# A decoder layer with sparse attention: DRAM scratch of queries, keys and compression in plain rows, keys stored once, the compression's places as extra matmul columns

## The chip, the core and the metric

One Trainium2 chip, of which the kernel uses one core. The metric is device time in microseconds (us) of one execution; the kernel before was timed in three runs. A profile of one more execution, taken by the hardware profiler, gives the rows below.

## The reference, cut to what matters

One decoder layer on 1024 tokens of width 1024: a projection of x to all mixers' inputs, a gated linear recurrence, a sparse attention with three branches, a gated merge, layer norm, a feed-forward part. The change touches the attention's inputs. Queries have 16 heads of 64; keys and values have 4 heads ("kv"), each for a group of 4 query heads. Queries and the three kinds of keys are rotated by position (rope), which mixes the two halves of 32 in each head. The compressed branch takes blocks of 32 tokens, 16 apart, adds a learned place to each token of the block and runs the block through a small network:

```python
def compress(t, pos_emb, w1, b1, w2, b2):
    ...
    blk = t[:, idx] + pos_emb[None, None, :, None, :]
    blk = blk.transpose(0, 1, 3, 2, 4).reshape(B, n_cmp, H, CMP_LEN * d)
    hdn = jax.nn.silu(blk @ w1 + b1)
    return hdn @ w2 + b2
```

It runs once for the keys (kind 0, on rotated keys) and once for the values (kind 1, not rotated).

## The kernel before, in words

All matmuls of the projections keep near-float32 precision by splitting each operand into a high and a low part of a reduced type: `split` (line 128) casts to the high part on ScalarE (ACT, line 118) and subtracts on VectorE (DVE, line 126); `mm3` (lines 142 to 145) then runs three matmuls, high by high, low by high and high by low. TensorE is PE; PEld are its weight loads.

**Phase 0** (to about 365 us) projects everything that is rotated or compressed. Activations are held transposed as `xh`, `xl`. `pair` loads one weight chunk of 1 MB (tile `w`, two buffers) and splits it to `wh`, `wl` (two buffers each). `rope` (line 273) makes, for each half of 512 tokens, two result tiles `pa` and `pb` of 24 matmuls each (first and second halves of the heads; two buffers each), four products with cosine and sine on VectorE (lines 283 to 286), two sums on GpSimd (POOL, lines 287 and 288), and hands the results to a sink:
- `sink_q` (line 298) splits them and stores four tiles `rh` of 256 KB to `Qd`. The 128 partitions of a tile are 4 heads by 32; in DRAM `Qd` is ordered kv, then 128 rows, then head, so the DRAM side of a store is a pattern of 4 x 32 x 512.
- `sink_k` (line 305) does the same for keys to `Kd`, ordered by kv, and stores each tile twice, so that a later load finds the key in both halves of the 128 partitions. The DRAM pattern is again 4 x 32 x 512, and one rotation makes 16 stores.
- `sink_c` puts the compression's input into `krt` in blocks; `compress_relay` (line 330) stores it to the scratch `Rd`, in four pieces of 256 KB for each kind (DRAM patterns 4 x 32 x 512 for kind 0, 2 x 64 x 512 for kind 1).

The compression of one kind has two halves a (first and second 16 tokens of a block). `compress_keys(kind, a)` (line 356) loads all of `Rd[kind]` (1 MB) into `kr`, adds the places of half a on VectorE (line 364, four instructions), and splits `kr` to `kh` and `kl`. `compress_hidden` (line 371) loads and splits half of the first weights and runs 48 matmuls of 256 columns into the result tiles `hps`. `compress_end` adds the bias, applies the activation and the second matmul. Each of `kr`, `kh`, `kl` has one buffer.

The order of phase 0 is written out (lines 441 to 483): values' and keys' compression inputs, keys(1, 0), rotation of the window keys kw, hidden(1, 0), keys(1, 1), rotation of the selected keys ks, hidden(1, 1), keys(0, 0), queries of kv 0, end(1), hidden(0, 0), keys(0, 1), gates, values vs, hidden(0, 1), values vw, end(0), queries of kv 1 to 3. That is the order of priority; the order on each engine's queue is then planned by the framework, which simulates the program with assumed durations. Every engine works its queue in order. All transfers are issued on the sync engine (SP), in order too: `dma` (line 135) for loads and `dmo` (line 140) for stores.

**Phase 1** (to about 1480 us) runs 32 attention units (4 kv by 8 tiles of 128 queries). `load_kv` (line 732) loads keys `K` (for each of two branches a tile of 128 partitions by 2 x 1024, in two transfers) and values `V` for one kv; `unit` (line 745) loads its queries `Q` (256 KB, two buffers) and computes scores `sc` (line 785). A filler puts the recurrence's matmuls (`pj`) between the units; its first part, `recurrence_values`, stores tiles `it` to `Id`. The tiles of phase 1 use memory that phase 0 releases. **Then** follow the merge, the output projection, norms and the feed-forward part.

Of the kernel before, what the change touches and what calls it, by code (L numbers as in the profile page):

```python
# [9 lines left out]
F32 = mybir.dt.float32  # L10
F32R = mybir.dt.float32r
I32 = mybir.dt.int32
AF = mybir.ActivationFunctionType
OP = mybir.AluOpType
AX = mybir.AxisListType

S = 1024
D = 1024
KT = D // 128
ST = S // 128  # L20
KV = 4
G = 4
# [87 lines left out]
def body(tc, xT, xS, pos, csa, csb, wA, wB, wG, lbl, normg, kpos, kw1, kb1, kw2, kb2, vpos, vw1, vb1,  # L110
# [17 lines left out]
    def split(hi, lo, src, e1="act", e2="dve"):  # L128

        copy(e1, hi, src)  # L130
        sub(e2, lo, src, hi.bitcast(F32))
# [5 lines left out]
    def dmo(o, i):  # L137

        o, i = (t.bitcast(F32) if t.dtype == F32R else t for t in (o, i))
        nc.sync.dma_start(o, i)  # L140

    def mm3(ps, ah, al, bh, bl, start, stop):
        nc.tensor.matmul(ps, ah, bh, start=start, stop=False)  # L143
        nc.tensor.matmul(ps, ah, bl, start=False, stop=False)  # L144
        nc.tensor.matmul(ps, al, bh, start=False, stop=stop)  # L145

    with ctx:
# [5 lines left out]
        nc.vector.memset(powc, -0.5)  # L153


        Qd = dram.tile([KV, 128, G, S], F32, name="Qd")
        Kd = dram.tile([2, KV, 2, 128, S], F32, name="Kd")
        Vd = dram.tile([8, 128, ST, 128], F32, name="Vd")
        Rd = dram.tile([2, 2, 64, KV, 512], F32, name="Rd")
        Id = dram.tile([HH, 128, ST, 128], F32, name="Id")  # L160
        Gd = dram.tile([2, 8, 128, S], F32, name="Gd")
        Md = dram.tile([8, 128, S], F32, name="Md")
# [32 lines left out]
        def pair(name, i=0):  # L195
            return chunk(wpa, wA[PAIRS[name, i]], 256)

        def token_rows(pool, name, w, s2):

            h, l = w  # L200
            p = pool.tile([128, 2, 256], F32, name=name)
            for j in range(2):
                sl = slice((s2 + j) * 128, (s2 + j) * 128 + 128)
                for k in range(KT):
                    mm3(p[:, j], xh[:, k, sl], xl[:, k, sl], h[:, k], l[:, k], k == 0, k == KT - 1)
            return p
# [4 lines left out]
        with p0:  # L211
# [86 lines left out]
            def sink_q(kv):  # L298
                def f(half, y1, y2):
                    sl = slice(half * 512, half * 512 + 512)  # L300
                    for c, y in enumerate(halves(y1, y2)):
                        dmo(Qd[kv, 32 * c:32 * c + 32, :, sl].rearrange("d h s -> h d s"), y)
                return f

            def sink_k(br):
                def f(half, y1, y2):
                    sl = slice(half * 512, half * 512 + 512)
                    for c, y in enumerate(halves(y1, y2)):
                        r0 = 32 * (c % 2)
                        for rep in range(2):  # L310
                            dmo(Kd[br, :, c // 2, r0 + 64 * rep:r0 + 64 * rep + 32, sl], y)
                return f


# [15 lines left out]
            def compress_relay(kind):  # L330

                for j in range(2):
                    for a in range(2):
                        if kind == 0:

                            o = Rd[0, a, 32 * j:32 * j + 32].rearrange("d k x -> k d x")
                        else:

                            o = Rd[1, a, :, 2 * j:2 * j + 2].rearrange("d k x -> k d x")
                        dmo(o, krt[j][:, a].rearrange("p r m -> p (r m)"))  # L340


            CM = [dict(posT=kpos, w1=kw1, b1=kb1, w2=kw2, b2=kb2), dict(posT=vpos, w1=vw1, b1=vb1, w2=vw2, b2=vb2)]
            W = KV * 512

            def compress_begin(kind):
                C = CM[kind]
                C["pt"] = a0.tile([128, 16], F32, name="cpos")
                nc.sync.dma_start(C["pt"], C["posT"])
                C["w2s"] = a0.tile([128, 2, 128], F32, name="w2s")  # L350
                nc.sync.dma_start(C["w2s"], C["w2"])
                C["b1s"] = a0.tile([128, 2], F32, name="b1s")
                nc.sync.dma_start(C["b1s"], C["b1"])
                C["hps"] = [ps0.tile([128, KV * 64], F32, name=f"hps{j}") for j in range(2)]

            def compress_keys(kind, a):

                C = CM[kind]
                kr = c0.tile([128, W + 8], F32, name="kr")
                nc.vector.memset(kr[:, W:], 0.0)  # L360
                nc.sync.dma_start(kr[:, :W], Rd[kind].rearrange("a d k x -> (a d) (k x)"))
                for kv in range(KV):
                    o = kr[:, kv * 512:kv * 512 + 512].rearrange("p (r m) -> p r m", r=8)
                    nc.vector.tensor_tensor(
                        o, o, C["pt"][:, 8 * a:8 * a + 8, None].to_broadcast([128, 8, 64]), op=OP.add)
                kh = c0.tile([128, W + 8], F32R, name="kh")
                kl = c0.tile([128, W + 8], F32R, name="kl")
                split(kh, kl, kr)
                C["k", a] = kh, kl

            def compress_hidden(kind, a):
                C = CM[kind]
                kh, kl = C["k", a]
                wh, wl = chunk(wpa, C["w1"][:, 8 * a:8 * a + 8], 256)

                def rhs(t, r):
                    o = r * 64 + a
                    return bass.AP(tensor=t.tensor, offset=t.offset + o,
                                   ap=[t.ap[0], [512, KV], [1, 64]])

                for r in range(8):
                    for j in range(2):
                        js = slice(j * 128, j * 128 + 128)
                        mm3(C["hps"][j], wh[:, r, js], wl[:, r, js], rhs(kh, r), rhs(kl, r),
                            a == 0 and r == 0, a == 1 and r == 7)

            def compress_end(kind):
# [2 lines left out]
                hid = a0.tile([128, 2, KV * 64], F32, name="hid")  # L390
                for j in range(2):
                    sg = a0.tile([128, KV * 64], F32, name="sg")
                    nc.vector.tensor_scalar(hid[:, j], hps[j], b1s[:, j:j + 1], None, op0=OP.add)
                    nc.scalar.activation(sg, hid[:, j], AF.Tanh, scale=0.5)
                    nc.vector.tensor_scalar(sg, sg, 0.5, 0.5, op0=OP.mult, op1=OP.add)
                    nc.vector.tensor_tensor(hid[:, j], hid[:, j], sg, op=OP.mult)
# [24 lines left out]

            c0 = p0.enter_context(tc.tile_pool(name="c0", bufs=1))


            def gate_chunk():
                w = wpa.tile([128, KT, 128], F32, name="wg", tag="w")
# [20 lines left out]
            rope("kc", 0, sink_c)  # L447
            compress_relay(0)
            compress_begin(1)
            compress_keys(1, 0)  # L450
            rope("kw", 0, sink_k(1))
            compress_hidden(1, 0)
            compress_keys(1, 1)
            rope("ks", 0, sink_k(0))
            compress_hidden(1, 1)
            compress_begin(0)
            compress_keys(0, 0)
            rope("nq", 0, sink_q(0))
            compress_end(1)
            compress_hidden(0, 0)  # L460
            compress_keys(0, 1)

            def values(name, i, evacuate):
                w = pair(name, i)
                for s2 in range(0, ST, 2):
                    evacuate(s2, token_rows(ps0, "pa" if s2 % 4 else "pb", w, s2))

            def sink_v(br):
                def f(s2, p):
                    vt = a2.tile([128, KV, 2, 128], F32R, name="vt", tag="vt", bufs=1)  # L470
                    p_ = p.rearrange("p t (c d) -> p c t d", d=64)
                    split(vt[:, :, :, :64], vt[:, :, :, 64:], p_)
                    dmo(Vd[4 * br:4 * br + 4, :, s2:s2 + 2].rearrange("c p t d -> p c (t d)"),
                        vt.rearrange("p c t d -> p c (t d)"))
                return f

            gate_chunk()
            values("vs", 0, sink_v(0))
            compress_hidden(0, 1)
            values("vw", 0, sink_v(1))  # L480
            compress_end(0)
            for kv in range(1, KV):
                rope("nq", kv, sink_q(kv))

# [247 lines left out]
        def load_kv(kv):  # L732
            r = {}
            for br in range(2):

                t = t1.tile([128, 2, S + 64 * br], F32R, name=f"K{br}")
                for c in range(2):
                    dma(t[:, c, :S], Kd[br, kv, c])
                r["k", br] = t
                t = t1.tile([128, ST, 128], F32R, name=f"V{br}")  # L740
                dma(t, Vd[br * 4 + kv])
                r["v", br] = t
            return r

        def unit(kv, qt, KV_):
            Q = t1.tile([128, G, 128], F32R, name="Q", bufs=2)
            dma(Q, Qd[kv, :, :, qt * 128:qt * 128 + 128])
            gt = lambda br: gates[:, qt, br * 16 + kv * 4:br * 16 + kv * 4 + 4]


# [462 lines left out]
```

## Time and profile before

| | us |
|---|---|
| median of 3 runs (lowest, highest) | 2421.12 (2420.8, 2422.0) |
| the profiled execution | 2419.0 |
| its span, first to last instruction | 2416.8 |
| PE busy | 2328.2 (96%) |
| DVE busy | 1344.2 (56%) |
| ACT busy | 890.6 (37%) |
| POOL busy | 572.4 (24%) |
| transfers moved | 204.45 MB, 85 GB/s in the mean |

Busy time is that of instructions that compute; the profiled execution's time is 2.2 us over its span. In tables by stretch of time, "x" counts instructions that started there, PEclk is TensorE's granted clock as a share of 2.4 GHz, and the DMA share is the busy share of the core's 16 DMA engines, with the rate beside it. In tables of waits a line says which engine at which line waited for whom: us in total, how often, the longest. "SPq" is the sync engine's queue, where a duration is that of issuing.

### The profile page before, as it was taken

Reading aid. Unit: us, or ns where it says so; the run is one execution under the profiler, and the core shown is the slowest. Engines: PE = TensorE matmul, PEld = TensorE weight load, DVE = VectorE, ACT = ScalarE, POOL = GpSimd, SP = SyncE. Lnnn points to the kernel's source line nnn. Section 1 sums busy time; section 2 is a strip of 40 time slices with the busy share of each in tenths; the row PEclk is TensorE's granted clock in tenths of the full one; section 3 lists DMA queues with packets and bytes.
Section 4 is the critical chain, followed back from the end, with each engine's and each line's share of the span. In section 5 each row is a group of like instructions: output and inputs, shape, how many; then the busy total and the mean of one; then the engine's idle time right before and its main releaser. Section 6 shows DMA issues by size and latency. Waiting matters only on the chain.

```text
span 2416.8 us, 32370 instructions
## 1 busy us (share of the span) xinstructions
PE 2328.2 (96%) x12068; PEld 1966.2 (81%) x12068; DVE 1344.2 (56%) x3474; ACT 890.6 (37%) x1573; POOL 572.4 (24%) x476
## 2 busy tenths in 40 slices
PE   8857989999999999999999999999999999999998
PEld 6747879988888888888888788887888888888886
DVE  4534436777777867676777965427333332323237
ACT  3212114556655655555655644213121211212020
POOL 0210112243444434443444531203000000000001
PEclk9978999999999999999999999999999999999999
DMA  5244341111311122111311435431111111211011
GB/s 203 108 175 148 120 175 53 56 61 53 107 64 42 58 71 101 51 58 55 110 57 31 162 125 189 153 135 57 53 53 44 62 44 36 70 35 61 20 59 70
DMA packets 99942, 204.45 MB, mean 85 GB/s; under 512 B 8650, under 2 KB 43850, under 8 KB 96842
## 3 DMA queue, kind: packets, MB, share of 16 engines
q1 hardware_dynamic: 99786, 202.40, 24.4%
q8 instruction: 95, 1.56, 0.3%
q14 instruction: 61, 0.50, 0.1%
HBM read 149.94 MB, written 52.43 MB: 84 GB/s over the span
## 4 chain that ended last, share of the span: by engine, by line
PE 85%; DVE 6%; DMA 5%; ACT 2%; SPq 1%; issue 1%; POOL 0%; DVEq 0%; ACTq 0%; POOLq 0%
PE pj L145 7%; PE pj L144 7%; PE pj L143 7%; PE sc L785 5%; PE pt L824 5%; PE pg L144 3%; PE pg L145 3%; PE pg L143 3%; PE pu L145 3%; PE pu L144 3%; PE pu L143 3%; PE pd L145 3%; PE pd L144 3%; PE pd L143 3%; PE pv L878 2%; PE pv L877 2%
## 5 line engine op out<-in xcount | busy, mean ns | idle before, releaser
L817 POOL TENSOR_TENSOR P<-P,sm 128x640 f32<-128x640 f32 (+6 forms) x192 | 206.3, 1077 | 330.8 <-DVE sm L813 234.4
L143 PE MATMUL pj<-xh,wh 128*128 128x512 f32 x640 | 257.5, 402 | 0.2 <-ACT wh L118 0.2
L144 PE MATMUL pj<-xl,wh 128*128 128x512 f32 x640 | 255.6, 399 | 0.0
L145 PE MATMUL pj<-xh,wl 128*128 128x512 f32 x640 | 255.5, 399 | 0.0
L807 ACT ACTIVATE P<-P,mx 128x640 f32<-128x640 f32 (+7 forms) x256 | 188.2, 736 | 177.4 <-DVE mx L805 174.5
L118 ACT CAST ph<-pt 128x512 fp32r<-128x512 f32 (+1 forms) x296 | 166.8, 583 | 166.1 <-PE pt L824 155.2
L785 PE MATMUL sc<-K,Q 128*128 128x352 f32 (+8 forms) x800 | 207.4, 346 | 13.2 <-DMA Id<-it 10.5
L118 ACT CAST wh<-w 128x1024 fp32r<-128x1024 f32 (+2 forms) x120 | 139.4, 1163 | 190.0 <-PE pg L144 72.6
L126 DVE TENSOR_TENSOR pl<-pt,ph 128x512 fp32r<-128x512 f32 x264 | 178.5, 685 | 44.4 <-ACT ph L118 43.0
L1023 POOL TENSOR_TENSOR rs<-rs,powc 128x1 f32<-128x1 f32 x16 | 11.9, 742 | 781.1 <-DVE rs L1022 781.1
L126 DVE TENSOR_TENSOR wl<-w,wh 128x1024 fp32r<-128x1024 f32 (+2 forms) x72 | 108.4, 1507 | 124.4 <-ACT wh L118 124.3
L824 PE MATMUL pt<-ca,P 128*128 128x128 f32 x1056 | 172.8, 272 | 0.1
L785 PEld LDWEIGHTS sc<-K,Q 128*128 128x128 f32 x800 | 134.2, 190 | 30.7 <-issue 12.9
L824 PEld LDWEIGHTS pt<-ca,P 128*128 128x128 f32 x1056 | 133.7, 140 | 28.2 <-DVE pl L126 0.3
L144 PE MATMUL pg<-mt,wh 128*128 128x512 f32 x352 | 138.7, 394 | 0.0
L143 PE MATMUL pg<-mt,wh 128*128 128x512 f32 x352 | 138.5, 393 | 0.0
L145 PE MATMUL pg<-mt,wl 128*128 128x512 f32 x352 | 138.5, 393 | 0.0
L145 PE MATMUL pu<-mt,wl 128*128 128x512 f32 x352 | 138.3, 393 | 0.0
L145 PEld LDWEIGHTS pj<-xh,wl 128*128 128x128 f32 x640 | 120.9, 189 | 21.3
L144 PE MATMUL pu<-mt,wh 128*128 128x512 f32 x352 | 138.2, 393 | 0.0
L143 PE MATMUL pu<-mt,wh 128*128 128x512 f32 x352 | 138.1, 392 | 0.0
L144 PEld LDWEIGHTS pj<-xl,wh 128*128 128x128 f32 x640 | 121.0, 189 | 20.4
(270 smaller groups left out, 5659.2 us busy)
## 6 DMA issues: line engine op xcount, KB each, us to landing
w<-in_wB_dram SPq DMA_DIRECT2D x40, 512.0 KB
w<-in_wA_dram SPq DMA_DIRECT2D x13, 1024.0 KB
w<-in_wfg_dram SPq DMA_DIRECT2D x22, 512.0 KB
w<-in_wfu_dram SPq DMA_DIRECT2D x22, 512.0 KB
w<-in_wfd_dram SPq DMA_DIRECT2D x22, 512.0 KB
Kd<-rh SPq DMA_DIRECT2D x32, 256.0 KB
Qd<-rh SPq DMA_DIRECT2D x32, 256.0 KB
K<-Kd SPq DMA_DIRECT2D x16, 512.0 KB
```

The source lines that it names most:

```text
L118: nc.scalar.copy(o, i)
L126: e.tensor_tensor(o, a, b, op=OP.subtract)
L143: nc.tensor.matmul(ps, ah, bh, start=start, stop=False)
L144: nc.tensor.matmul(ps, ah, bl, start=False, stop=False)
L145: nc.tensor.matmul(ps, al, bh, start=False, stop=stop)
L785: nc.tensor.matmul(ps[:, :wx], Q[:, g], KV_["k", br][:, c_, ks], start=c_ == 0, stop=c_ == 1)
L807: nc.scalar.activation(P[:, :nk], P[:, :nk], AF.Exp, scale=-1.0, bias=mx[:, g, npc - 1:npc], accum_out=den[:, g:g + 1])
L817: nc.gpsimd.tensor_tensor(P[:, :nk], P[:, :nk], cg.to_broadcast([128, nk]), op=OP.mult)
L824: nc.tensor.transpose(pt[:n, g * 128:g * 128 + 128], src[:, g], ident)
L877: nc.tensor.matmul(pv, v, ph, start=i == 0, stop=False)
L878: nc.tensor.matmul(pv, v, pl, start=False, stop=i == len(tiles) - 1)
L1023: nc.gpsimd.tensor_tensor(rs, rs, powc, op=OP.pow)
```

## The change

Scratch in DRAM: `Qd` is stored as [kv, c, 128, S], `Kd` as [branch, c, 128, S], once, and `Rd` as [kind, j, 128, 2, 512], each written as 128 rows. The loads do the reordering: four key pieces of 32 partitions for each branch, four query pieces of 32 partitions for each unit, four pieces of `kr` for each kind. `compress_keys` runs once per kind. The places are no longer added to the keys: they stand as extra columns of `kh` and `kl`, and each hidden matmul has 4 x 66 columns in place of 4 x 64; `compress_end` adds the column that results to the bias. The order of phase 0 becomes: keys(1), kw, hidden(1, 0), hidden(1, 1), ks, end(1), keys(0), queries of kv 0, hidden(0, 0), hidden(0, 1), gates, vs, end(0), vw, queries of kv 1 to 3.

```diff
-        Qd = dram.tile([KV, 128, G, S], F32, name="Qd")
-        Kd = dram.tile([2, KV, 2, 128, S], F32, name="Kd")
+        Qd = dram.tile([KV, 4, 128, S], F32, name="Qd")
+        Kd = dram.tile([2, 4, 128, S], F32, name="Kd")
-        Rd = dram.tile([2, 2, 64, KV, 512], F32, name="Rd")
+        Rd = dram.tile([2, 2, 128, 2, 512], F32, name="Rd")
...
-                        dmo(Qd[kv, 32 * c:32 * c + 32, :, sl].rearrange("d h s -> h d s"), y)
+                        dmo(Qd[kv, c, :, sl], y)
...
-                        r0 = 32 * (c % 2)
-                        for rep in range(2):
-                            dmo(Kd[br, :, c // 2, r0 + 64 * rep:r0 + 64 * rep + 32, sl], y)
+                        dmo(Kd[br, c, :, sl], y)
...
-                    for a in range(2):
-                        if kind == 0:
-
-                            o = Rd[0, a, 32 * j:32 * j + 32].rearrange("d k x -> k d x")
-                        else:
-
-                            o = Rd[1, a, :, 2 * j:2 * j + 2].rearrange("d k x -> k d x")
-                        dmo(o, krt[j][:, a].rearrange("p r m -> p (r m)"))
+                    dmo(Rd[kind, j], krt[j].rearrange("p a r m -> p a (r m)"))
...
-                C["hps"] = [ps0.tile([128, KV * 64], F32, name=f"hps{j}") for j in range(2)]
-
-            def compress_keys(kind, a):
+                C["hps"] = [ps0.tile([128, KV, 66], F32, name=f"hps{j}") for j in range(2)]
+
+            def compress_keys(kind):
 
                 C = CM[kind]
-                kr = c0.tile([128, W + 8], F32, name="kr")
-                nc.vector.memset(kr[:, W:], 0.0)
-                nc.sync.dma_start(kr[:, :W], Rd[kind].rearrange("a d k x -> (a d) (k x)"))
+                kr = c0.tile([128, KV, 512], F32, name="kr")
+                for a in range(2):
+                    if kind == 0:
+
+                        for j in range(2):
+                            o = 64 * a + 32 * j
+                            nc.sync.dma_start(kr[o:o + 32], Rd[0, j, :, a].rearrange("(k d) x -> d k x", k=KV))
+                    else:
+
+                        for j in range(2):
+                            nc.sync.dma_start(kr[64 * a:64 * a + 64, 2 * j:2 * j + 2],
+                                              Rd[1, j, :, a].rearrange("(k d) x -> d k x", k=2))
+                kh = c0.tile([128, KV, 8, 68], F32R, name="kh")
+                kl = c0.tile([128, KV, 8, 68], F32R, name="kl")
+                k4 = kr.rearrange("p k (r m) -> p k r m", r=8)
+                split(kh[:, :, :, :64], kl[:, :, :, :64], k4)
+                places = C["pt"].rearrange("p (a r) -> p r a", a=2)[:, :, None, :].to_broadcast([128, 8, 2, 2])
                 for kv in range(KV):
-                    o = kr[:, kv * 512:kv * 512 + 512].rearrange("p (r m) -> p r m", r=8)
-                    nc.vector.tensor_tensor(
-                        o, o, C["pt"][:, 8 * a:8 * a + 8, None].to_broadcast([128, 8, 64]), op=OP.add)
-                kh = c0.tile([128, W + 8], F32R, name="kh")
-                kl = c0.tile([128, W + 8], F32R, name="kl")
-                split(kh, kl, kr)
-                C["k", a] = kh, kl
+                    h, l = (t[:, kv, :, 64:].rearrange("p r (t a) -> p r t a", a=2) for t in (kh, kl))
+                    split(h, l, places)
+                C["k"] = kh, kl
...
-                        mm3(C["hps"][j], wh[:, r, js], wl[:, r, js], rhs(kh, r), rhs(kl, r),
+                        mm3(C["hps"][j], wh[:, r, js], wl[:, r, js],
+                            kh[:, :, r, a:a + 66], kl[:, :, r, a:a + 66],
                             a == 0 and r == 0, a == 1 and r == 7)
...
-                    nc.vector.tensor_scalar(hid[:, j], hps[j], b1s[:, j:j + 1], None, op0=OP.add)
+                    h3 = hid[:, j].rearrange("p (k m) -> p k m", k=KV)
+                    nc.vector.tensor_tensor(b1s[:, j:j + 1], b1s[:, j:j + 1], hps[j][:, 0, 64:65], op=OP.add)
+                    nc.vector.tensor_scalar(h3, hps[j][:, :, :64], b1s[:, j:j + 1], None, op0=OP.add)
...
             compress_begin(1)
-            compress_keys(1, 0)
+            compress_keys(1)
             rope("kw", 0, sink_k(1))
             compress_hidden(1, 0)
-            compress_keys(1, 1)
-            rope("ks", 0, sink_k(0))
             compress_hidden(1, 1)
             compress_begin(0)
-            compress_keys(0, 0)
+            rope("ks", 0, sink_k(0))
+            compress_end(1)
+            compress_keys(0)
             rope("nq", 0, sink_q(0))
-            compress_end(1)
             compress_hidden(0, 0)
-            compress_keys(0, 1)
+            compress_hidden(0, 1)
             gate_chunk()
             values("vs", 0, sink_v(0))
-            compress_hidden(0, 1)
+            compress_end(0)
             values("vw", 0, sink_v(1))
-            compress_end(0)
...
-                for c in range(2):
-                    dma(t[:, c, :S], Kd[br, kv, c])
+                for rep in range(2):
+                    for j in range(2):
+                        o = 64 * rep + 32 * j
+                        dma(t[o:o + 32, :, :S], Kd[br, j::2, 32 * kv:32 * kv + 32].rearrange("c d s -> d c s"))
...
-            dma(Q, Qd[kv, :, :, qt * 128:qt * 128 + 128])
+            for c in range(4):
+                dma(Q[32 * c:32 * c + 32],
+                    Qd[kv, c, :, qt * 128:qt * 128 + 128].rearrange("(g d) s -> d g s", g=G))
```

## Rows read from the trace of the kernel before

**Rows 1.** Busy time by stretch: PE, PEld, DVE, ACT, POOL (instructions); clock, DMA.
```profile
31.00:60.00 29.00, 29.00 (x129) 24.01 (x129) 7.03 (x7) 7.49 (x9) 0.00 (x0) 1.00 0.32 121
...
60.00:64.60 4.60, 0.44 (x2) 0.02 (x1) 3.13 (x6) 0.00 (x0) 0.55 (x1) 0.82 0.13 52
64.60:70.00 5.40, 5.38 (x13) 4.26 (x14) 4.63 (x4) 4.10 (x6) 2.42 (x2) 0.52 0.00 0
...
117.00:135.50 18.50, 0.15 (x2) 0.00 (x0) 0.00 (x0) 1.90 (x1) 0.00 (x0) 0.61 0.60 232
135.50:152.00 16.50, 8.34 (x18) 5.18 (x19) 12.52 (x16) 3.36 (x4) 4.56 (x2) 0.51 0.26 101
...
178.40:199.70 21.30, 5.90 (x14) 4.22 (x14) 10.89 (x15) 5.61 (x8) 3.48 (x2) 0.60 0.44 152
...
354.50:365.00 10.50, 0.06 (x1) 0.00 (x0) 1.69 (x1) 0.00 (x0) 0.00 (x0) 0.60 1.00 355
365.00:371.00 6.00, 5.95 (x29) 5.98 (x30) 1.67 (x8) 1.51 (x3) 1.25 (x1) 0.57 0.20 68
```

**Rows 2.** Waits of PE from 371 to 1480 us, the longest.
```profile
PE sc L785 <- DVE mx L805: 2.6, 3, 1.4
```

**Rows 3.** Waits of PE from 0 to 380 us, the three longest.
```profile
PE pa L143 <- ACT wh L118: 18.4, 1, 18.4
PE pa L145 <- DVE wgl L126: 11.4, 1, 11.4
PE sc L785 <- DMA Id<-it: 10.5, 1, 10.5
```

**Rows 4.** Waits of all engines from 0 to 370 us: two that end in transfers.
```profile
DVE kr L364 <- DMA kr<-Rd: 83.4, 4, 36.6
...
ACT wh L118 <- DMA w<-in_wA_dram: 35.2, 5, 28.4
```

**Rows 5.** The sync queue in order of time, 75 to 180 us: start, us, what.
```profile
82.18 37.92 SPq L140 DMA_DIRECT2D Kd<-rh  x16
...
124.84 44.10 SPq L140 DMA_DIRECT2D Kd<-rh  x16
...
171.45 1.31 SPq L135 DMA_DIRECT2D wg<-in_wG_dram  x1
```

**Rows 6.** Chain that ended last, in order of time: start, us, what.
```profile
40.58 15.97 DMA Rd<-krt
...
56.68 4.76 DMA kr<-Rd
...
335.14 15.02 DMA Qd<-rh
```

**Rows 7.** Busy time by stretch, as rows 1: loads, value scratch stores, key stores.
```profile
16.00:24.00 8.00, 8.00 (x37) 6.62 (x36) 7.67 (x10) 4.57 (x5) 0.00 (x0) 1.00 1.04 405
...
46.00:56.00 10.00, 10.00 (x46) 8.28 (x45) 0.00 (x0) 0.00 (x0) 0.00 (x0) 1.00 0.13 51
...
102.00:112.00 10.00, 10.00 (x50) 8.44 (x49) 0.42 (x1) 1.24 (x2) 2.51 (x2) 1.00 0.26 102
```

**Rows 8.** Instructions on kr: ns minimum/median/maximum, first and last start us, forms.
```profile
L364 DVE TENSOR_TENSOR kr<-kr,cpos x16: 681/684/1381, 61.5 to 188.8; 128x512 f32<-128x512 f32 x16
...
L118 ACT CAST kh<-kr x4: 1905/1910/1914, 65.9 to 199.4; 128x2056 fp32r<-128x2056 f32 x4
L126 DVE TENSOR_TENSOR kl<-kr,kh x4: 2293/2295/2299, 67.8 to 201.7; 128x2056 fp32r<-128x2056 f32 x4
```

**Rows 9.** Busy PE of matmuls into hps, one hidden half; clock, DMA.
```profile
83.40:89.20 5.80, 5.70 (x48) 1.00 0.28 104
```

**Rows 10.** Query loads on the sync queue, columns as in rows 8.
```profile
L135 SPq DMA_DIRECT2D Q<-Qd x32: 524/560/606, 355.0 to 1423.4; - x32
```

**Rows 11.** The sync queue in order of time, 10 to 20 us.
```profile
12.52 0.43 SPq L349 DMA_DIRECT2D cpos<-in_vpos_dram  x1
13.70 0.33 SPq L351 DMA_DIRECT2D w2s<-in_vw_dram  x1
```

More of the change, by code (lines that the diff above doesn't have):

```diff
@@ L332, in compress_relay @@
                 for j in range(2):
-                    for a in range(2):
-                        if kind == 0:
-                            o = Rd[0, a, 32 * j:32 * j + 32].rearrange("d k x -> k d x")
-                        else:
-                            o = Rd[1, a, :, 2 * j:2 * j + 2].rearrange("d k x -> k d x")
-                        dmo(o, krt[j][:, a].rearrange("p r m -> p (r m)"))
+                    dmo(Rd[kind, j], krt[j].rearrange("p a r m -> p a (r m)"))
             CM = [dict(posT=kpos, w1=kw1, b1=kb1, w2=kw2, b2=kb2), dict(posT=vpos, w1=vw1, b1=vb1, w2=vw2, b2=vb2)]
-            W = KV * 512
             def compress_begin(kind):
@@ L371, in compress_hidden @@
             def compress_hidden(kind, a):
                 C = CM[kind]
-                kh, kl = C["k", a]
+                kh, kl = C["k"]
                 wh, wl = chunk(wpa, C["w1"][:, 8 * a:8 * a + 8], 256)
[L376 to L379, printed above, removed]
                 for r in range(8):
@@ L422, in body, with values, sink_v, f @@
             c0 = p0.enter_context(tc.tile_pool(name="c0", bufs=1))
+            def values(name, i, evacuate):
+                w = pair(name, i)
+                for s2 in range(0, ST, 2):
+                    evacuate(s2, token_rows(ps0, "pa" if s2 % 4 else "pb", w, s2))
+            def sink_v(br):
+                def f(s2, p):
+                    vt = a2.tile([128, KV, 2, 128], F32R, name="vt", tag="vt", bufs=1)
+                    p_ = p.rearrange("p t (c d) -> p c t d", d=64)
+                    split(vt[:, :, :, :64], vt[:, :, :, 64:], p_)
+                    dmo(Vd[4 * br:4 * br + 4, :, s2:s2 + 2].rearrange("c p t d -> p c (t d)"),
+                        vt.rearrange("p c t d -> p c (t d)"))
+                return f
             def gate_chunk():
@@ L449, in body @@
             compress_begin(1)
-            compress_keys(1, 0)
+            compress_keys(1)
             rope("kw", 0, sink_k(1))
             compress_hidden(1, 0)
-            compress_keys(1, 1)
-            rope("ks", 0, sink_k(0))
             compress_hidden(1, 1)
             compress_begin(0)
-            compress_keys(0, 0)
+            rope("ks", 0, sink_k(0))
+            compress_end(1)
+            compress_keys(0)
             rope("nq", 0, sink_q(0))
-            compress_end(1)
             compress_hidden(0, 0)
-            compress_keys(0, 1)
[L463 to L475, printed above, removed]
+            compress_hidden(0, 1)
             gate_chunk()
             values("vs", 0, sink_v(0))
-            compress_hidden(0, 1)
+            compress_end(0)
             values("vw", 0, sink_v(1))
-            compress_end(0)
             for kv in range(1, KV):
```

## The prediction

> **What bounds the kernel now.** I read the busy time by stage first, then TensorE's own waits, then who keeps those others waiting, then the sync engine's queue of transfers. TensorE (PE) is busy 96% of the span, so time can be had only where it stands still or where its clock is low. The stages [rows 1] show four such places, all in the first 371 us. A matmul of 512 columns takes 29.0/129 = 0.225 us at granted clock 1.00, in the undisturbed stretch; at about 0.5, the lower of the two levels (1.2 of 2.4 GHz), it takes about twice that, and the clock is low in and after each of the long idle spells.
> - A (60 to 70 us): 4.6 - 0.44 idle, then 13 matmuls in 5.4 us where 13 x 0.225 = 2.9 would do: lost 4.2 + 2.5 = 6.7 us.
> - B (117 to 152): 18.5 - 0.15 idle, then 18 matmuls in 16.5 us where 4.05 would do: lost 18.35 + 12.45 = 30.8 us.
> - C (178.4 to 199.7): 14 matmuls in 21.3 us where 3.15 would do: lost 18.1 us.
> - E (354.5 to 371): 10.4 idle, then 6.0 us at mean clock 0.57, 6.0 x 0.43 = 2.6 lost: 13.0 us.
>
> Together 68.6 us. From 371 to 1480 us TensorE waits for nothing that counts: the longest entry adds up to 2.6 us [rows 2].
>
> At B, C and E TensorE names as releasers a weight cast on ScalarE (18.4), the gate weights' subtraction on VectorE (11.4) and a transfer (10.5) [rows 3]. One step behind, VectorE stands 83.4 us, four times, in the addition of line 364 until the compression's keys are back from DRAM, and ScalarE 35.2 us until weights land [rows 4]. One more step behind is the queue that carries both: from 82 to 120 us the sync engine issues nothing but 16 stores of the window keys, 37.92 us or 2.37 each; from 125 to 169 the 16 of the selected keys; only then, at 171.45, the gate weights [rows 5]. So B and C are the queue of key stores, A is the store of the compression's scratch (15.97 us), and E is the last query store (15.02 us), until whose end the memory for phase 1's keys and queries is not free [rows 6].
>
> **Why those stores are slow** stands in the transfer columns [rows 7]. Loads of 128 plain rows: share 1.04, 405 GB/s. Key stores, whose DRAM side is written as 4 x 32 rows: 0.26, 102 GB/s, a quarter of the 16 engines. Scratch stores of the value kind, written as 2 x 64 rows: 0.13, 51 GB/s, an eighth. The share follows the count of the DRAM pattern's slowest dimension, 4/16 and 2/16.
>
> **The change, part by part.**
> 1. Plain rows: Qd, Kd and Rd are written as 128 rows. 256 KB then costs between 2.37 us (as now) and 256 KB at 405 GB/s = 0.65 us; I take 0.65, the loads of 128 rows being the same shape. Both ends stay for the rivals.
> 2. Keys stored once: 32 key stores become 16. Per branch 16 x 2.37 = 38 us of queue become 8 x 0.65 = 5 us. **B** loses its cause: the weights that could start only at 120 us leave about 30 us sooner, and the second load of the keys, behind which the rotation's products stood on VectorE up to 140 us, is gone. I take back all 30.8.
> 3. One key load per kind where there were two, as four pieces of 256 KB, and no addition ahead of the split. The wait for the keys does not vanish: the cast to the high half on ScalarE takes it. **A**: the last scratch store leaves at 40.6 and the load behind it took 4.8 [rows 6]. With 4.8 for the store too, a high end, the keys are there at 50.2; cast 1.9 and subtraction 2.3 [rows 8] end at 54.4, before 60, where TensorE runs out of result buffers. All 6.7 come back.
> 4. **C**: the gate weights leave when their buffer is free, and the fourth key load is gone. The first load of the key kind remains, but a whole rotation (96 matmuls of 0.225, 21.6 us) lies between it and its matmuls. All 18.1 come back.
> 5. **E**: the last query store leaves at 335.1; four of 0.65 us without a backlog are down by about 338.3. The loads took 14.8 us from the store's end to the first scores (350.2 to 365.0), so 353.1, before 354.5. Against this: they are cut into more pieces (K from 4 to 8 per head group, Q from 1 to 4). At full rate E is gone (13.0). At half rate for the 2 MB of K and 0.5 MB of Q, 2.62e6 bytes at 405 GB/s = 6.5 us more, the scores start at 359.6, 5.1 idle and 2.6 of clock remain, 5.3 are saved. I take 10, nearer the full rate, at which every load row here runs.
> 6. A new tight place: the two halves of each hidden layer now stand next to each other. One half is 5.7 us of matmuls [rows 9], and in it the next weights must be cast (1.9) and subtracted (2.3, both as in rows 8), beside the rotation's own work. Between 0 and 6 us of new idle for each of the two kinds; I take 2 each: **-4**.
> 7. Wider matmuls: 4 halves of 5.7 us, 264 columns for 256: -0.7.
> 8. VectorE loses 16 additions of 0.68 and two subtractions of 2.3, some 15 us, ScalarE two casts of 1.9 [rows 8]; 8 casts and 8 subtractions of 32 columns (2056 take those times) and four additions of one column come in. From 31 to 60 us both are busy a quarter of the time [rows 1]: nothing for the sum; uncovered it would be some 12 us in favour.
> 9. The sync queue gets 96 more query issues of 0.56 us [rows 10] and 16 more of keys, some 60 us over 1100. Queries are fetched a unit ahead, and TensorE waits for no transfer there [rows 2]: nothing; without that cover see the last rival.
>
> Sum: 6.7 + 30.8 + 18.1 + 10 - 4 - 0.7 = 60.9 us. The profiled execution took 2419.0 (span 2416.8), which gives 2358.1; the median of the runs, 2421.1, lies 2.1 higher: **2360**.
>
> The Trainium skill speaks against part 5: SBUF — State Buffer, section "Door 1: The DMA port swizzle (why `[64,N]` ≈ `[32,N]`)", says that a transfer's rate depends on how many of the 16 ports its partitions reach, and 32 partitions reach 8. No row of this trace shows a piece of 32 partitions; by that rule it would be the half rate above, as in the first rival.
>
> **Rivals.**
> - *Pieces of 32 partitions run at half rate* (18%). For it: nothing in the trace moves such pieces, so nothing excludes it. Against: the shares seen follow the count of rows, and 32 is over 16. E gives 5.3 in place of 10: 2365.
> - *ScalarE inherits the wait* (12%). For it: ScalarE holds every weight cast, and TensorE already stood 18.4 us behind one; a cast of keys that comes too early in its order blocks the weights behind it, once per kind. A key load takes 4.8 us, the low clock after it 2.5 as in A: 2 x 7.3 = 15 us: 2375. Against: the queue that made the loads late is gone.
> - *Stores stay at a quarter rate* (5%), because something else sets 102 GB/s. Halving their count still clears B and C; A and E stay: 30.8 + 18.1 - 4.7 = 44 us: 2377. Against: 0.26 and 0.13 beside 1.04.
> - *The stalls only move* (2%): the order on each engine is planned with assumed times and may open the same holes elsewhere: 2421.
> - *Query pieces choke the queue* (3%), the case that ends slower. Place: phase 1, 32 units. Two small loads near 13 us are issued 1.2 us apart [rows 11], since the later one waits for a transfer ahead. If each of three added pieces cost 1.2 us and nothing of it were hidden, 32 x 3 x 1.2 = 115 us: 2475. It decides against the change when a unit exposes over 61/32 = 1.9 us. Against: two query buffers, and no wait for a transfer there [rows 2].
>
> **How the numbers follow.** The forecast has 60%. Everything returned and no new stall gives 68.6 - 0.7 = 67.9: 2353; phase 1, whose order is planned anew, may move some us either way, so the range starts at 2347. Upwards it takes in the half rate, ScalarE's wait, and the quarter rate with part 6 at its upper end (8 more than taken: 2385). Left out of 2347 to 2385 are the last two rivals and what I have not thought of. A measurement of this kernel tells about 0.2% (5 us) from no change; every case but the last two lies far below it: faster 0.95, same 0.02, slower 0.03.
>
> **What would show it.** Right: during the key stores the transfer share stands near 1.0 in short bursts, not at 0.26; the sync queue has no block of 16 stores; the wait for the keys' return, 83.4 us on VectorE, is under 15 on ScalarE; TensorE idles under 15 us from 31 us to the first scores, which start near 305 in place of 365. Part 5 is told by the idle right ahead of those scores: under 1 us, or about 5. Wrong: idle of over 5 us behind a cast of keys (second rival) or at the change from one hidden half to the next (part 6), or scores that wait for queries later (the slower case).

## The result, and the profile after

The changed kernel takes 2362.8 us (median of 4 runs, 2359.8 to 2364.2) where the kernel before, beside it, takes 2421.0: a ratio of 0.976, 95% interval 0.974 to 0.977. The forecast was 2360, the range 2347 to 2385. The profiled execution took 2362.05 us (span 2359.7); that of before 2419.0 (2416.8), so the difference to be explained is 57.0 us.

TensorE's own waits up to 360 us are read first, all that there are: engine, tile, line, releaser, then us in total, times, longest.

```profile
PE sc L784 <- DMA Id<-it: 9.0, 1, 9.0
PE pa L143 <- ACT xh L118: 6.8, 3, 5.3
PE pj L143 <- DVE rt L287: 1.5, 1, 1.5
```

Of [rows 3] the two waits of B and C (18.4 behind the weight cast, 11.4 behind the gate weights' subtraction) are gone; the third, at E, stands at 9.0 where it was 10.5. The 6.8 is at the program's start, before 12 us.

The stages, with the columns of [rows 1]. First all from 12 to 276 us in one row, then a stretch of it with key stores behind each other and one with a single key store, then what is left of E.

```profile
12.00:276.00 264.00, 262.53 (x1446) 228.86 (x1445) 132.10 (x151) 76.84 (x94) 48.94 (x28) 1.00 0.45 155
...
74.00:76.00 2.00, 2.00 (x10) 1.69 (x9) 0.00 (x0) 0.00 (x0) 0.00 (x0) 1.00 1.04 393
...
80.00:81.00 1.00, 1.00 (x10) 1.00 (x9) 1.00 (x2) 0.00 (x0) 1.00 (x1) 1.00 0.64 248
...
298.50:307.60 9.10, 0.09 (x1) 0.01 (x1) 1.96 (x1) 0.00 (x0) 0.00 (x0) 0.66 0.95 228
307.60:312.00 4.40, 4.38 (x20) 4.40 (x21) 1.67 (x8) 1.51 (x3) 0.49 (x1) 0.54 0.32 101
```

Through A, B and C TensorE is now busy 262.53 of 264 us at granted clock 1.00: 6.7 + 30.8 + 18.1 = 55.6 us are back. Key stores behind each other have a share of 1.04 and 393 GB/s, where 10 us of them had 0.26 and 102 [rows 7]. The single store, issued at 79.52, keeps the 16 engines busy for 0.64 of 1 us: the 0.65 us that the prediction took for 256 KB. E is still there: 9.1 - 0.09 = 9.0 idle, and 4.4 us at 0.54, 4.4 x 0.46 = 2.0: 11.0 lost where 13.0 were lost before. 55.6 + 2.0 = 57.6 against the 57.0 of the two profiled executions.

Next the sync queue, as in [rows 5] (start, us, what), and behind it the waits on transfers of the engines that fed B and C, as in [rows 4].

```profile
68.65 14.48 SPq L140 DMA_DIRECT2D Kd<-rh  x6
83.23 0.81 SPq L135 DMA_DIRECT2D w<-in_wA_dram  x1
84.13 0.86 SPq L140 DMA_DIRECT2D Kd<-rh  x2
...
117.10 0.39 SPq L135 DMA_DIRECT2D wg<-in_wG_dram  x1
...
278.01 0.38 SPq L135 DMA_DIRECT2D w<-in_wA_dram  x1
278.49 0.87 SPq L140 DMA_DIRECT2D Qd<-rh  x2
```

```profile
ACT wh L118 <- DMA w<-in_wA_dram: 11.7, 5, 5.7
ACT kh L118 <- DMA kr<-Rd: 11.3, 1, 11.3
```

The block of 16 stores in 37.92 us is gone. Where two key stores stand with their data ready, they are issued in 0.86 us; the 14.48 for six is the pace of the rotation that makes the data. Weights follow at 83.23, and the gate weights leave at 117.10, not at 171.45. ScalarE waits 11.7 us for weights, not 35.2. VectorE's 83.4 us behind the compression's keys are gone, and ScalarE's cast of them waits 11.3 in their place.

The chain that ended last, around E, as in [rows 6]:

```profile
278.98 8.20 DMA Qd<-rh
...
287.77 5.13 DMA K<-Kd
...
292.92 11.64 DMA K<-Kd
...
304.63 2.83 DMA Id<-it
...
307.62 1.51 PE sc L784 x4
```

The last query store takes 8.20 us, not 15.02; a weight load of 1 MB was issued just ahead of it, at 278.01. It stood there in the kernel before too, 1.2 us ahead of the last query store:

```profile
333.92 0.46 SPq L135 DMA_DIRECT2D w<-in_wA_dram  x1
```

The loads behind the store take 307.6 - 287.2 = 20.4 us to the first scores, where they took 14.8. These two are what is left of E. The wait ahead of the scores is put down to a store `Id<-it`, issued behind the loads; the scores need the queries, whose loads stand behind those of K and V in the queue.

### The profile page after: what moved, and what is told of

Its sections match the earlier page's. It is cut to its first block, busy times and chain, and to the rows that moved or that the text cites. A ratio compares the mean times of both kernels' runs of the same rounds, so it can differ in the third digit from the quotient of the medians.

```text
span 2359.7 us, 32494 instructions
## 1 busy us (share of the span) xinstructions
PE 2319.0 (98%) x12068; PEld 1962.8 (83%) x12068; DVE 1334.1 (57%) x3464; ACT 887.5 (38%) x1579; POOL 572.7 (24%) x476
## 4 chain that ended last, share of the span: by engine, by line
PE 89%; DVE 5%; DMA 3%; ACT 1%; issue 1%; POOL 0%; SPq 0%; DVEq 0%; ACTq 0%; POOLq 0%
PE pj L144 7%; PE pj L143 7%; PE pj L145 7%; PE sc L784 5%; PE pt L823 5%; PE pg L144 3%; PE pg L145 3%; PE pg L143 3%; PE pu L145 3%; PE pu L144 3%; PE pu L143 3%; PE pd L145 3%; PE pd L144 3%; PE pd L143 3%; PE pv L877 2%; PE pv L876 2%
```

## The experiments

Two things were open: which part of the change had closed B, C and A (the spread of each store over the engines, the halved count, or the compression's own edit), and why E had stayed. Each edit below is to the changed kernel, unless another is named; all times are medians, with the ratio's 95% interval against the kernel before that ran beside them (2420.4 to 2421.7 us).

### Keys as 4 x 32 rows, still stored once

```
- Kd = dram.tile([2, 4, 128, S]);     dmo(Kd[br, c, :, sl], y)
+ Kd = dram.tile([2, 4, KV, 33, S]);  dmo(Kd[br, c, :, :32, sl], y)
```

The 33rd row keeps the four groups of 32 apart, so that the store is written as 4 x 32 again.

> The changed kernel, except that each key store's DRAM side is again 4 x 32 rows (one spare row between the groups), still stored once. Theory 'spread' (the slowest dimension of the DRAM pattern sets how many of the 16 transfer engines work): in the key stores the transfer share is 0.26 and 102 GB/s again, 8 stores take 19 us where 8 plain ones take 5, the weights behind them come 5 to 10 us later and TensorE stands still in phase 0: 5 to 20 us over the changed kernel's 2363, so 2368 to 2383. Rival 'bytes' (the gain came from halving the number of key stores): 2363, within 5.

Measured: 2361.6 us, 0.975 (0.974 to 0.977), against the theory. The stores were slow again:

```profile
76.00:80.00 4.00, 4.00 (x29) 3.77 (x28) 2.17 (x3) 2.33 (x2) 1.74 (x2) 1.00 0.26 102
```

Yet no wait of TensorE came back. The spread of the rows alone had not been needed: eight slow stores a branch still fit into the time that the queue has.

### Queries as 4 x 32 rows

```
- Qd = dram.tile([KV, 4, 128, S]);    dmo(Qd[kv, c, :, sl], y)
+ Qd = dram.tile([KV, 4, G, 33, S]);  dmo(Qd[kv, c, :, :32, sl], y)
```

> The changed kernel, except that each query store's DRAM side is again 4 x 32 rows (one spare row between the groups). Theory 'spread': share 0.26 in the query stores; the last one ends 5 to 8 us later, and all of it goes into the idle ahead of the first scores, 9.0 us in the changed kernel: 14 to 17 here, 2368 to 2372. Rival (the last store is late because a 1 MB weight load is ahead of it, not because of its pattern): idle stays near 9, 2363 within 4.

Measured: 2368.6 us, 0.978 (0.977 to 0.980), 5.8 us above the changed kernel. The chain that ended last in this run:

```profile
280.28 14.98 DMA Qd<-rh
...
314.10 1.51 PE sc L784 x4
```

The last query store takes 14.98 us again, nearly the 15.02 of [rows 6], and the first scores start 6.5 us later. At E the plain rows of the queries are worth this much: without them TensorE's wait there is 14.5 us, longer than the 10.5 of before.

### Plain rows, but the keys stored twice

```
  dmo(Kd[br, c, :, sl], y)
+ dmo(Ke[br, c, :, sl], y)
```

> The changed kernel, with each key tile stored a second time in plain rows to a scratch that nobody reads. Theory 'spread': 16 more stores of 0.65 us, some 10 us of queue in two places where TensorE has its weights already: 2363, within 4. Rival 'bytes': the halving counted for about as much as the plain rows; the 8 more stores for each branch hold the weights back again: 2370 or more.

Measured: 2361.3 us, 0.976 (0.974 to 0.977). From 104 to 119 us the transfers have a share of 0.57 and 212 GB/s (0.37 and 122 in the changed kernel), and no wait of TensorE came back. Storing them once had not been needed either, once each store is spread.

### Both taken back: 4 x 32 rows, stored twice

```
+ dmo(Kd[br, c, :, :32, sl], y)
+ dmo(Ke[br, c, :, :32, sl], y)
```

> The changed kernel with both old faults of the key stores at once: DRAM side of 4 x 32 rows, and each tile stored a second time, to a scratch that nobody reads. Each fault by itself changed nothing (2361.6 and 2361.3). Theory 'slack' (16 stores at 2.4 us are 38 us of queue, 8 at 2.4 are 19 and 16 at 0.65 are 10; the weights behind them are needed about 20 us after the first store): only both together exceed it, TensorE stands 10 us or more behind a weight cast, twice, 2385 to 2410. Rival (the key stores had nothing to do with it): 2362 within 4.

Measured: 2392.1 us, 0.988 (0.987 to 0.989), 29 us above the changed kernel. TensorE's waits, a stretch of this run's sync queue, and the same place in the chain that ended last:

```profile
PE hps L413 <- DVE hid L396: 11.8, 2, 10.4
PE pa L143 <- ACT wgh L118: 9.8, 1, 9.8
```

```profile
101.73 2.44 SPq L140 DMA_DIRECT2D Ke<-rh  x1
104.22 2.41 SPq L135 DMA_DIRECT2D w<-in_wA_dram  x1
```

```profile
104.22 13.26 DMA w<-in_wA_dram
117.56 1.91 ACT wh L118
```

Each store holds the queue for about 2.4 us again, and the weight load behind them does too. The load then lands 13.26 us after its issue; ScalarE casts it at 117.56, and VectorE subtracts it only then, ahead of the `hid` that TensorE waits for. So there is a threshold in this kernel: 8 x 2.4 = 19 us of slow stores a branch cost nothing, 16 x 2.4 = 38 us cost 29 us in all. The change came back below it twice over, by the layout and by the count, and with its new compression either was enough. With the old compression the two were only run together, in the next experiment.

### The layouts alone

The kernel before with the plain rows of queries, keys and scratch, keys stored once and loaded in pieces; its compression, with two loads of the keys and an addition for each half, is left as it was.

```
- Kd = dram.tile([2, KV, 2, 128, S])
+ Kd = dram.tile([2, 4, 128, S])
- nc.sync.dma_start(kr[:, :W], Rd[kind].rearrange("a d k x -> (a d) (k x)"))
+ for a_ in range(2):
+     for j in range(2):
+         nc.sync.dma_start(kv_[...], Rd[kind, j, :, a_]...)
```

> The kernel before with plain rows and keys stored once, but with the compression's keys still loaded twice for each kind, the places still added on VectorE, and the old order. Theory 'queue' (the prediction's: A, B and C are the slow stores ahead of weights and keys): TensorE's idle in phase 0 is gone, 2363 to 2372. Rival 'single load' (what emptied phase 0 is that the second key load and VectorE's wait for it are gone): VectorE still waits 20 us or more for keys, 2375 to 2395.

Measured: 2359.8 us, 0.975 (0.973 to 0.976), the whole gain. Waits of this run:

```profile
DVE kr L366 <- DMA kr<-Rd: 26.2, 4, 9.6
```

```profile
PE sc L791 <- DMA Id<-it: 8.5, 1, 8.5
```

VectorE still stands 26.2 us behind the keys, in four waits (83.4 before), but none of it reaches TensorE, whose only long wait in these stages is the one at E.

### The compression's edit alone

The changed kernel with the three old layouts, their stores and their loads: keys twice as 4 x 32, scratch as before, one load of 1 MB for the compression's keys.

```
- Qd = dram.tile([KV, 4, 128, S])
+ Qd = dram.tile([KV, 128, G, S])
- Kd = dram.tile([2, 4, 128, S])
+ Kd = dram.tile([2, KV, 2, 128, S])
- Rd = dram.tile([2, 2, 128, 2, 512])
+ Rd = dram.tile([2, 2, 64, KV, 512])
```

> The kernel before with the compression of the changed kernel alone (keys loaded once for each kind, places as columns, the new order), all layouts and the doubled key stores as before. Theory 'queue': 16 stores of 2.4 us for each kind of keys still hold the weights back; TensorE stands 15 us or more in phase 0 and 10 or more ahead of the first scores: 2390 to 2410. Rival 'single load': phase 0 is clear and only the last query store's place remains: 2368 to 2376.

Measured: 2427.7 us (10 runs, 2420.8 to 2432.4), 1.003 (1.0015 to 1.0039): slower by 0.3%, and outside every expectation. The stages A and B of this run, then TensorE's longest waits, then its sync queue:

```profile
60.00:70.00 10.00, 10.00 (x46) 8.29 (x45) 4.76 (x4) 6.40 (x8) 2.06 (x2) 1.00 0.15 62
117.00:135.50 18.50, 0.00 (x0) 0.00 (x0) 0.00 (x0) 0.00 (x0) 0.00 (x0) 0.50 0.44 145
```

```profile
PE hps L410 <- DVE hid L393: 37.6, 2, 36.2
PE pa L143 <- ACT wgh L118: 10.7, 1, 10.7
PE sc L779 <- DMA Q<-Qd: 10.2, 1, 10.2
```

```profile
84.89 42.13 SPq L140 DMA_DIRECT2D Kd<-rh  x16
127.06 3.35 SPq L135 DMA_DIRECT2D w<-in_wA_dram  x1
```

The block of 16 stores is back, now 42.13 us long, and the weights behind it leave at 127.06. So the edit does not spare TensorE the late weights: one wait alone is 36.2 us, and the time is no better than before. But A is gone, with the old scratch: 46 matmuls from 60 to 70 us at clock 1.00.

### The old scratch alone

```
- Rd = dram.tile([2, 2, 128, 2, 512])
+ Rd = dram.tile([2, 2, 64, KV, 512])
- dmo(Rd[kind, j], krt[j].rearrange("p a r m -> p a (r m)"))
+ for a in range(2):
+     dmo(o, krt[j][:, a].rearrange("p r m -> p (r m)"))
```

The scratch is laid out and loaded as before (one load of 1 MB), with one load per kind and the cast behind it.

> The changed kernel with the compression's scratch in the old layout (stores of 2 x 64 and 4 x 32 rows, one whole load for each kind). Theory (place A was the slow store of the value kind): that store takes 16 us again, the keys come 10 us later than the 51.6 of the changed kernel, ScalarE's cast and VectorE's subtraction end at about 66, TensorE runs out of result buffers at 60: 4 to 7 us idle and 2.5 of low clock, 2368 to 2372. Rival (with the cast on ScalarE, VectorE's products no longer stand behind the keys): 2362 within 4.

Measured: 2360.9 us, 0.975 (0.973 to 0.976). The load of the keys is issued only at 57.17, behind the slow scratch stores, ScalarE's cast waits 22.09 us for them, and still TensorE does not stop:

```profile
60.00:70.00 10.00, 10.00 (x46) 8.28 (x45) 4.91 (x4) 6.56 (x8) 2.21 (x2) 1.00 0.14 56
```

```profile
57.17 0.33 SPq L357 DMA_DIRECT2D kr<-Rd  x1
```

VectorE does not escape the wait: its subtraction stands behind ScalarE's cast. What changed is where in VectorE's order the wait stands. The last products of the rotation ahead of the wait, and the instruction that ends it, in the kernel before and then in this run:

```profile
41.03 0.68 DVE L284 TENSOR_TENSOR rt<-pa,sinT 128x512 f32<-128x512 f32 x1
61.47 1.90 DVE L364 TENSOR_TENSOR kr<-kr,cpos 128x512 f32<-128x512 f32 x3 [19.76 <-DMA kr<-Rd]
```

```profile
50.61 0.68 DVE L285 TENSOR_TENSOR rt<-pa,sinT 128x512 f32<-128x512 f32 x1
64.81 2.29 DVE L126 TENSOR_TENSOR kl<-kr,kh 128x2048 fp32r<-128x2048 f32 x1 [13.53 <-ACT kh L118]
```

In the kernel before, VectorE takes up no product between 41.7 and 61.5 us; here it has read two more result tiles, up to 51.3, before it stands, and TensorE could go on filling them. So A, too, had two cures in this change. Either the keys come earlier (the run with the layouts alone), or they come late and VectorE meets the wait after more of its products (this run, and the one before it). That this order is all that keeps TensorE going was not tested by itself.

### E: loads of 128 partitions in place of 32

The key and query loads take whole tiles of 128 partitions. The scores are then of rows in a wrong order; the volume, the count of matmuls and their shapes are the same.

```
- dma(t[o:o + 32, :, :S], Kd[br, j::2, 32 * kv:32 * kv + 32]...)     # 4 of them
+ dma(t[:, c, :S], Kd[br, c + 2 * (kv % 2)])                         # 2
- dma(Q[32 * c:32 * c + 32], Qd[kv, c, :, qt * 128:qt * 128 + 128]...)  # 4
+ dma(Q, Qd[kv, :, :, qt * 128:qt * 128 + 128].rearrange("c p s -> p c s"))
```

> The changed kernel, with keys loaded by two transfers of 128 partitions for each branch and queries by one, straight from the rows as they lie (the scores are then of wrongly ordered rows; sizes and counts of bytes as in the changed kernel). Theory 'pieces' (a piece of 32 partitions moves at about half the rate of one of 128): the rate ahead of the first scores rises from 217 to 252 GB/s to 350 or more, the idle there falls from 9.0 us to under 4, 2354 to 2359. Rival (the loads are late only because the last query store ends late, and they are more than they look): rate and idle stay, 2363 within 4.

Measured: 2358.5 us, 0.974 (0.972 to 0.975). The stretch of the loads, from the end of the last query store to about the first scores, in this run, in the changed kernel, and in the next experiment:

```profile
287.00:302.00 15.00, 12.30 (x103) 12.09 (x101) 2.29 (x1) 2.49 (x2) 0.29 (x1) 1.00 0.89 310
```

```profile
287.00:307.00 20.00, 11.59 (x97) 11.39 (x95) 2.29 (x1) 2.49 (x2) 0.29 (x1) 0.86 0.95 233
```

```profile
287.00:305.00 18.00, 12.00 (x101) 11.80 (x99) 2.29 (x1) 2.49 (x2) 0.29 (x1) 0.90 0.95 259
```

The same volume, 4.65 to 4.66 MB (us times GB/s), takes 15.0 us whole and 20.0 in pieces of 32, with the 16 engines busy 0.89 and 0.95 of the time. From 290 to 300 us the rates are 361 and 249 GB/s, a factor of 0.69, at shares of 0.99 and 1.04. But that stretch mixes the pieces with loads of 128 partitions, such as V. From 291.5 to 296 us, when the load of a table ahead of them (`cs`, in by 291.6) is done and V stands behind them in the queue, the first four key pieces are nearly alone. The changed kernel, then this run in the same stretch:

```profile
291.50:296.00 4.50, 4.50 (x40) 4.50 (x39) 0.00 (x0) 0.00 (x0) 0.00 (x0) 1.00 1.06 218
```

```profile
291.50:296.00 4.50, 4.50 (x40) 4.50 (x39) 0.00 (x0) 0.31 (x1) 0.00 (x0) 1.00 0.98 369
```

The pieces move 218 GB/s, 0.59 of the 369 here and 0.54 of the 405 of [rows 7]. The share alone would have shown no difference: the engines were busy all the time at little over half of the rate. TensorE's idle time at E falls from 9.0 to 3.0 us, and the first scores start at 302.33, 5.3 us earlier. The median is 4.3 us lower; the two intervals overlap.

### Pieces that alternate between the partition halves

```
- for rep in range(2): for j in range(2):   # K
+ for j in range(2): for rep in range(2):
- for c in range(4):                        # Q
+ for c in (0, 2, 1, 3):
```

> The changed kernel, with the pieces of 32 partitions issued alternately for the lower and the upper 64 partitions (keys 0, 64, 32, 96; queries likewise). Theory 'ports' (a piece is slow because all engines write to the same half of the ports, so that neighbours in the queue from both halves can share the time): rate ahead of the first scores above 300 GB/s, idle there under 6.5 us, 2357 to 2361. Rival (each engine works its pieces in order and all are at the same one): rate and idle stay, 2363 within 3.

Measured: 2361.6 us, 0.975 (0.974 to 0.977). The stretch takes 18.0 us (the third row above); from 290 to 300 us the rate is 277 GB/s, and while key pieces are nearly alone, from 291.5 to 295, it is 246 for 218. The wait ahead of the scores falls from 9.0 to 6.6 us. That is a gain of about a tenth in rate, less than the theory asked for and more than the rival. The time is not told apart from that of the changed kernel.

### Loads in the order in which phase 1 wants them

```
- for br in range(2):
+ for br in (1, 0):
+ Q = load_q(kv, qt)          # ahead of the loads of K and V, was in unit()
```

> The changed kernel, with the first loads of phase 1 in another order: queries and window keys (which the first scores read) ahead of the selected keys and both values. Theory (the idle ahead of the first scores is the time of some 4 MB of loads behind the last query store, of which the scores need a third): the first scores start 8 to 10 us sooner, the idle of 9.0 us and the low clock after it go: 2350 to 2355. Rival (the memory comes free too late, whatever is loaded first): idle above 6 us, 2360 to 2363.

Measured: 2364.0 us, 0.976 (0.975 to 0.978), no gain, near the rival's time; but its reason, an idle time that stays above 6 us, fails. The first scores start 9.4 us earlier than in the changed kernel, after an idle time of 4.6 us:

```profile
298.25 1.51 PE sc L787 x4
```

E falls from 11.0 to about 7.4 us (4.6 idle, and from the first scores on 12.0 us at mean clock 0.77, 12.0 x 0.23 = 2.8). That is not 9.4: the work before the loads' end was put off, not done. And what was won there is not in the end time. Near the end of phase 1, first this run, then the changed kernel:

```profile
1300.00:1420.00 120.00, 114.25 (x569) 93.65 (x570) 80.07 (x275) 58.22 (x128) 52.46 (x47) 0.99 0.42 133
```

```profile
1300.00:1420.00 120.00, 117.86 (x595) 97.85 (x595) 87.78 (x285) 60.57 (x134) 53.32 (x47) 0.98 0.43 133
```

In this stretch TensorE is busy 3.6 us less and runs 26 matmuls fewer. Phase 1 has work of other kinds that its plan lets TensorE do in between; with another start it left other holes. That these holes are the whole of the loss was not shown, and the 3.6 us that E gained are within the 4.3 us by which the changed kernel's own runs differ.

### Both of the last two

```
+ the order of the loads, and the alternating pieces
```

> The changed kernel with both edits of the loads ahead of the first scores: queries and window keys first, pieces for the lower and upper partitions in turn. Idle there falls from 9.0 us to 4 or less. Theory 'worth what it shows' (every us of that idle is a us of the time): 2352 to 2357. Rival 'given back' (an earlier first score only moves filler matmuls, and the order planned for phase 1 changes with it; the load order alone gave 2364.0): 2359 to 2365.

Measured: 2361.7 us, 0.975 (0.974 to 0.977), first scores at 297.67 after a wait of 5.0 us. E shrinks, the time doesn't, as the rival had it.

### Pieces on the store side

Keys are stored in the order in which phase 1 reads them, so that its loads take 128 partitions; each store becomes eight of 64 KB.

```
- dmo(Kd[br, c, :, sl], y)
+ for rep in range(2):
+     for kv in range(KV):
+         dmo(Kd[br, kv, c // 2, r0 + 64*rep : r0 + 64*rep + 32, sl], y[32*kv : 32*kv + 32])
```

> The changed kernel with keys stored as the load wants them, twice, in pieces of one head (32 rows, 64 KB, 64 stores for each kind of keys), and loaded by two whole transfers of 128 partitions for each branch. Theory 'pieces': the load's gain of the run with whole loads comes back with correct keys, idle ahead of the first scores 9.0 falls to 5 or less; the 64 stores take 21 us of issuing, which the slack of phase 0 holds: 2356 to 2361. Rival: the pieces only move to the store's side, where 64 stores from 32 partitions take 25 us or more for each kind and hold weights back: 2368 or more.

Measured: 2377.4 us, 0.982 (0.980 to 0.983), 14.6 us slower than the change. TensorE's longest waits behind the start, and this run's sync queue:

```profile
PE hps L143 <- ACT wh L118: 11.5, 1, 11.5
...
PE sc L786 <- DMA Q<-Qd: 2.4, 1, 2.4
```

```profile
68.62 32.70 SPq L140 DMA_DIRECT2D Kd<-rh  x64
101.85 0.45 SPq L135 DMA_DIRECT2D w<-in_wA_dram  x1
```

E is down to a wait of 2.4 us, but 64 stores hold the queue for 32.7 us and the weight load behind them leaves at 101.85, not at 83.23: B comes back in part. In this kernel the pieces cost less where the loads are.

## Why the prediction was right, point by point

- **Parts 2, 3 and 4, the places B, A and C: right, in the sum and in the place.** All 55.6 us came back. The queue of key stores was the cause at B and C: the run that brings it back in the changed kernel (both taken back) loses 29 us of their 48.9, one wait behind a late weight load and one behind the gate weights. The run with all old layouts as well loses the whole gain.
- **What the prediction did not see** is that each place had more cures than it needed. It gave B to the spread and the halving together (38 us of queue to 5); either alone would have done, because the queue has room for 19 us of stores a branch. It gave A to the earlier keys of part 3; the compression's edit alone does it too. Beside the layouts that edit added nothing that can be measured: without it they take 2359.8 us.
- **Part 3's moved wait: right.** ScalarE waits 11.3 us for the keys, under the 15 that were named, and TensorE does not stop behind it. The rival by which ScalarE inherits the stall falls.
- **Part 5, E: mis-sized, 10 us taken and 2 measured.** Two terms failed, by about as much each. "Down by about 338.3", 3.2 us from the last query store's issue, was 8.2 (and four stores of 0.65 make 2.6, not 3.2). The words "without a backlog" were wrong: from 278 to 287 us 9 us x 234 GB/s = 2.1 MB moved, of which the weight load is 1.05 MB, and the row of the kernel before with that load at 333.92, shown above, could have told it. That the weight load alone makes the store late was not tested. And the loads took 20.4 us, not the 14.8 of full rate; half rate for the pieces had been put at 14.8 + 6.5 = 21.3. The two errors, 5.0 and 5.6 us, less the 1.4 us of slack that the prediction had (354.5 - 353.1), are 9.2 against the 9.0 idle. So the first rival, which I gave 18%, had half of it: by the prediction's own test (idle under 1 or about 5) E went its way, and further, since the store came later too. The experiment with whole loads shows the rival's half, with 218 GB/s in pieces against 369.
- The rule weighed at part 5, in the Trainium skill, SBUF — State Buffer, section "Door 1: The DMA port swizzle (why `[64,N]` ≈ `[32,N]`)", says that a transfer's rate depends on how many of the 16 ports its partitions reach. The trace agrees, and nearly in the size that the prediction drew from it, a half: 218 GB/s for pieces of 32 partitions is 0.54 of the 405 of loads of 128.
- **Part 6, 4 us of new idle: did not come.** From 12 to 276 us there is no wait of TensorE over 1.5 us, and none at the hidden halves. This error is the opposite of part 5's and half its size, so the sum (60.9 taken, 57.0 measured) looks better than its terms: with 2 for part 5 and nothing for part 6 it is 55.6 + 2 - 0.7 = 56.9.
- **Parts 7 and 8** are too small to be told apart in these runs. The run with the layouts alone, which has neither, is no slower.
- **Part 9: right.** From 312 to 1425 us TensorE's longest wait is 2.3 us, for ScalarE, and none is for a transfer; the slower rival falls.
- The total does not choose between the forecast (2360) and the first rival (2365): 2362.8 lies between. At E the rival was nearer; that the forecast still came out within 3 us is luck, since its error there was covered in part by the 4 us of part 6.

## What to carry to other kernels

Look at the transfer share of a store before its bytes: written to DRAM as 4 or 2 outer groups it had 0.26 or 0.13 of the engines, as 128 plain rows 1.04, and the loads behind it in the queue paid. In this kernel such a cost had a threshold, so a part of the change could be worth 29 us or nothing depending on what else was shortened: undo each part alone, and then both. And what an earlier start of a long stage is worth depends on how it is won: first scores 5.3 us earlier by faster loads gave 4.3 us, 6.5 us later by slow stores cost 5.8, but 9.4 us earlier by the order of the loads alone gave nothing.

## What was not expected of the hardware

- A transfer share near 1 did not mean full rate: pieces of 32 partitions moved 218 GB/s at a share of 1.06 where loads of 128 moved 369 at 0.98. The order of the pieces alone raised it to 246.
- A store of 64 KB on 32 partitions held the sync queue 32.70/64 = 0.51 us in the mean, a store of 256 KB in plain rows 0.86/2 = 0.43: here a quarter of the size did not make a store shorter on the queue.
- A slow store holds what comes after it as well: the weight load behind the 4 x 32 stores took 2.41 us to issue where it took 0.81 behind plain ones.
